# Scaling the exponentials of three attentions on GpSimd instead of on ScalarE and VectorE in turn

## The chip, the cores and the metric

The kernel runs on one core of a Trainium2 chip. The metric is the device time of one execution in microseconds (us), the median of several runs. The engines are PE (TensorE, matmuls and transposes; PEld is its weight load), DVE (VectorE), ACT (ScalarE), POOL (GpSimd) and SP (SyncE, which issues most DMAs). Each engine works through its own instructions in a fixed order and waits at semaphores for the others.

## What is computed

Two layers of a first block and one layer of a second block run over a sequence of 256 positions with 1024 features. The layers hold five kinds of softmax attention, each over 256 causal positions. What matters here is the last step of a softmax: each row of exponentials is multiplied by one factor.

```python
s = jnp.einsum('bqhd,bkhd->bhqk', qs, k).astype(jnp.float32) * scale
p = jax.nn.softmax(jnp.where(causal, s, -jnp.inf), axis=-1)
return jnp.einsum('bhqk,bkhd->bqhd', p.astype(v.dtype), v)
```

The factor is one over the sum of the row. In the second block's first attention (its branches over selected and windowed positions) it is that times a gate, `gt[:, :, 1] * o_s + gt[:, :, 2] * o_w`, which the kernel folds into the same factor.

## The kernel before

Positions lie on the 128 partitions, in two halves. The scores of one head are a tile of 128 x 384: the first 128 columns are the first 128 queries against the first 128 keys, the other 256 columns are the second 128 queries against all keys. Each half has its own row sums, so each head has two factors per partition and two multiplications, of 128 x 128 and of 128 x 256.

Heads go in pairs. For a pair, `pair_scores` (L598) makes two banks of scores on PE (L603, L612). `softmax_rows` (L314) adds the bias or mask and takes the row maximum on DVE (L315), then ACT takes the exponential and the row sums (L316). DVE makes the factors (a reciprocal at L728, L1230 or L1249, and at L1231 a product with the gates). `scaled` (L545) multiplies the exponentials with their factors in place and hands the tile to `transposed` (L578): three transposes on PE into the one bank `pt` (L271 through `tr`), and a copy to SBUF on ACT (`ptsb`, L586). `pair_values` (L555) multiplies with the values on PE (L559, L561), and `put_pair` splits the result in a high and a low part on ACT (L540) and DVE (L541).

`scaled` counts its calls in `mix`. Calls with an even count use ACT (L550), the others DVE (L552), so of each pair one head goes to DVE and the other to ACT. It is called for 48 heads: by `attend` (L716) twice in each of the first block's two layers, for three pairs each time (24 heads); in the second block's gated attention (L1218 to L1235, eight pairs, 16 heads); and in its last attention (L1240 to L1252, four pairs, 8 heads). The differential attention between (L765 to L783) does not call it.

The tile `e` of the exponentials has four buffers, `ptsb` three, `pt` one bank and the scores two banks. The scores of a pair wait until DVE has read those of the pair before (`last_read`).

Beside the attentions, the same engines prepare weights: a matmul of the projections is done in three passes with a high and a low part of each operand (`mm3`, L274 to L278), and each weight tile is split by ACT (L129) and DVE (L130). The layout library orders the instructions of each engine by priorities and its own estimates; `high_priority` blocks move scores and values ahead. The projections' and the output projection's matmuls (`acc`) fill PE between the steps of the pairs. GpSimd so far only makes reciprocal square roots (L309 to L312) and a few small clears. Its queue issues no DMA.

Of the kernel before, what the change touches and what calls it, by code (L numbers as in the profile page):

```python
# [12 lines left out]
AF = mybir.ActivationFunctionType  # L13
OP = mybir.AluOpType
# [157 lines left out]
def body(ctx: ExitStack, tc: tile.TileContext, io, out):  # L172
    nc = tc.nc
    V, A, G, T = nc.vector, nc.scalar, nc.gpsimd, nc.tensor
# [365 lines left out]
        A.activation(dst[0], src, AF.Copy)  # L540
        V.tensor_tensor(dst[1], src, dst[0].bitcast(F32), op=OP.subtract)  # L541

    mix = [0]

    def scaled(e, r, ap):  # L545

        mix[0] += 1
        for t, c in ((0, slice(0, 128)), (1, slice(128, 384))):
            if mix[0] % 2 == 0:
                A.activation(e[:, c], e[:, c], AF.Copy, scale=r[:, t:t + 1])  # L550
            else:
                V.tensor_scalar(e[:, c], e[:, c], r[:, t:t + 1], None, op0=OP.mult)  # L552
        return transposed(e, ap, False)

    def pair_values(o, pts, v, c0, first, last):  # L555
# [22 lines left out]
    def transposed(e, ap, eng):  # L578
        b = bank2()
        for i in range(3):  # L580
            tr(b[:, i * 128:(i + 1) * 128], e[:, i * 128:(i + 1) * 128])
        pt = ap.tile([128, 384], F32, tag="ptsb", name="ptsb", bufs=3)
        if eng:
            V.tensor_copy(pt, b[:, :384])
        else:
            A.activation(pt, b[:, :384], AF.Copy)  # L586
        return pt
# [27 lines left out]
    def softmax2(s, bm, ap, sm):  # L615

        e = ap.tile([128, 384], F32, tag="e", name="e", bufs=4)
        nm = small(2)
        softmax_rows(e[:, 0:128], s[:, 0:128], bm[:, 128:256], nm[:, 0:1], sm[0])
        last_read.append(softmax_rows(e[:, 128:384], s[:, 128:384], bm, nm[:, 1:2], sm[1]))  # L620
        return e
# [17 lines left out]
    def hybrid(l, xres, xT, inc, inbv, early, next_entry, hooks):  # L639
        lam0 = 0.8 - 0.6 * math.exp(-0.3 * l)  # L640
        with tc.tile_pool(name=f"at{l}", bufs=1, reuse_waits="tile") as ap:
# [74 lines left out]
            def attend(q_of, k_of, bm_of, v, k0, hook=None):  # L716

                for j in range(3):
                    if j == PUTB and hook is not None:
                        hook()  # L720
                    o = obank2()
                    hs = (2 * j, 2 * j + 1)
                    ss = pair_scores(lambda h: q_of(hs[h]), lambda h: k_of(hs[h]))
                    pts = []
                    for i, s in zip(hs, ss):
                        sm = small(4)
                        e = softmax2(s, bm_of(i), ap, (sm[:, 0:1], sm[:, 1:2]))
                        V.reciprocal(sm[:, 2:4], sm[:, 0:2])  # L728
                        pts.append(scaled(e, sm[:, 2:4], ap))
                    pair_values(o, pts, v, (64 * hs[0], 64 * hs[1]), True, True)  # L730
                    put_pair(hdT, k0 + j, o)
# [221 lines left out]
    with tc.tile_pool(name="at2", bufs=1, reuse_waits="tile") as ap:  # L953
# [264 lines left out]
        for j in range(4):  # L1218
            if j == 2:
                dq = dsa_queries()  # L1220
            o = obank2()
            T.matmul(o, vcD[:, 2 * (j % 2):2 * (j % 2) + 2, :].rearrange("p s c -> p (s c)"), cp[:, j // 2, :],
                     start=True, stop=False)
            for br in range(2):
                ss = pair_scores(lambda h: nq[64 * h:64 * h + 64, j, :], lambda h: kSW[64 * h:64 * h + 64, br, :])
                pts = []
                for h in range(2):
                    sm = small(4)
                    e = softmax2(ss[h], mask, ap, (sm[:, 0:1], sm[:, 1:2]))
                    V.reciprocal(sm[:, 2:4], sm[:, 0:2])  # L1230
                    V.tensor_tensor(sm[:, 2:4], sm[:, 2:4], gw[:, :, 8 * (1 + br) + 2 * j + h], op=OP.mult)  # L1231
                    pts.append(scaled(e, sm[:, 2:4], ap))
                    next(top, None)
                pair_values(o, pts, vSW, (128 * (1 + br), 128 * (1 + br) + 64), False, br == 1)
            put_pair(hdT, j, o)  # L1235
# [4 lines left out]
        for j in range(4):  # L1240
            o = obank2()
            ss = pair_scores(lambda h: dq[64 * h:64 * h + 64, j, :], lambda h: kD[64 * h:64 * h + 64, j, :])
            pts = []
            for sc in ss:
                sm, nm = small(4), small(2)
                e = ap.tile([128, 384], F32, tag="e", name="e", bufs=4)
                softmax_rows(e[:, 0:128], sc[:, 0:128], sel[:, 0:128], nm[:, 0:1], sm[:, 0:1])
                last_read.append(softmax_rows(e[:, 128:384], sc[:, 128:384], sel[:, 128:384], nm[:, 1:2], sm[:, 1:2]))
                V.reciprocal(sm[:, 2:4], sm[:, 0:2])  # L1249
                pts.append(scaled(e, sm[:, 2:4], ap))  # L1250
            pair_values(o, pts, vD, (128 * j, 128 * j + 64), True, True)
            put_pair(hdT, 4 + j, o)  # L1252
# [117 lines left out]
```

## Time and profile before

| | |
|---|---|
| median of three runs | 978.37 us (977.81 to 980.41) |
| the profiled execution | 977.63 us |
| its span, first to last instruction | 975.8 us |
| PE busy | 944.4 us (97%) |
| DVE busy | 650.5 us (67%) |
| ACT busy | 533.2 us (55%) |
| POOL busy | 29.2 us (3%), 54 instructions |
| mean granted TensorE clock | 0.993 |

The profiled execution took 0.74 us less than the median, and 1.83 us lie outside its span. A busy share is an average over stages with different limits. Matmuls are pipelined, so a busy PE is not a PE at its peak: a matmul's record lasts longer than the distance to the next one's start. A row of the view by stretches gives, for each engine, the busy time and the number of its instructions (x) within that stretch; a row of the timeline gives start, duration, engine, line, operation, tiles, shape and, in brackets, the idle time before it and what ended that.

### The profile page before, as it was taken

How to read it: one execution, taken by the hardware profiler on the slowest of the kernel's cores; microseconds unless marked ns; L12 is line 12 of the kernel's file. 1: busy time of each engine (PE TensorE's matmuls, PEld its weight loads, DVE VectorE, ACT ScalarE, POOL GpSimd, SP SyncE). 2: the span in 40 equal slices, each digit the busy share in tenths (PEclk: the TensorE clock that was granted, in tenths of full speed). 3: DMA queues.
4: the chain of work that ended last, by engine and by line, in shares of the span. 5: the costliest groups of instructions: out<-in, count | busy, mean ns of one | idle time of the engine just before them, and what ended most of it. 6: DMA issues, size and time to landing. Idle time of an engine off the chain costs nothing. (4 is left out here: it accounts for less than half of the span.)

```text
span 975.8 us, 16344 instructions
## 1 busy us (share of the span) xinstructions
PE 944.4 (97%) x6378; PEld 834.9 (86%) x6378; DVE 650.5 (67%) x1367; ACT 533.2 (55%) x1023; POOL 29.2 (3%) x54
## 2 busy tenths in 40 slices
PE   8999999999999999999999999889999899999997
PEld 6888689999998888878999999788666699999996
DVE  4648687767678757767767464787688665454543
ACT  4658665444444677655444444555599744344542
POOL 0000000000000100000000000101000100000000
PEclk9999999999999999999999999999999999999999
DMA  8745548877875533447875565365312156555441
GB/s 313 288 100 215 196 176 301 300 278 270 300 254 175 192 131 127 149 179 278 308 277 211 177 242 190 109 242 206 130 45 87 65 173 215 175 181 205 153 153 44
DMA packets 33456, 190.55 MB, mean 195 GB/s; under 512 B 3696, under 2 KB 5346, under 8 KB 15842
## 3 DMA queue, kind: packets, MB, share of 16 engines
q1 hardware_dynamic: 31224, 183.75, 52.9%
q10 hardware_dynamic: 2154, 5.75, 2.0%
q8 instruction: 50, 0.82, 0.3%
q14 instruction: 28, 0.23, 0.1%
HBM read 188.17 MB, written 1.32 MB: 194 GB/s over the span
## 5 line engine op out<-in xcount | busy, mean ns | idle before, releaser
L130 DVE TENSOR_TENSOR lo<-raw,hi 128x1024 fp32r<-128x1024 f32 (+3 forms) x284 | 339.1, 1202 | 99.7 <-ACT hi L129 95.6
L129 ACT ACTIVATE hi<-raw 128x1024 fp32r<-128x1024 f32 (+3 forms) x284 | 293.7, 1041 | 103.1 <-PE acc L278 52.3
L278 PE MATMUL sc<-xh,lo 128*128 128x256 f32 x960 | 271.8, 283 | 0.0
L276 PE MATMUL sc<-xh,hi 128*128 128x256 f32 x960 | 271.7, 283 | 0.0
L277 PE MATMUL sc<-xl,hi 128*128 128x256 f32 x960 | 271.7, 283 | 0.0
L276 PEld LDWEIGHTS sc<-xh,hi 128*128 128x128 f32 x960 | 184.2, 192 | 1.1
L277 PEld LDWEIGHTS sc<-xl,hi 128*128 128x128 f32 x960 | 184.2, 192 | 1.0
L278 PEld LDWEIGHTS sc<-xh,lo 128*128 128x128 f32 x960 | 184.2, 192 | 0.0
L276 PE MATMUL acc<-hi,xh 128*128 128x512 f32 (+4 forms) x384 | 135.2, 354 | 0.4 <-ACT hi L129 0.3
L277 PE MATMUL acc<-lo,xh 128*128 128x512 f32 (+4 forms) x384 | 134.0, 349 | 0.7 <-DVE lo L130 0.6
L278 PE MATMUL acc<-hi,xl 128*128 128x512 f32 (+4 forms) x384 | 133.6, 349 | 0.7 <-DVE xl L298 0.7
L276 PE MATMUL acc<-hi,hh 128*128 128x512 f32 x264 | 103.2, 391 | 0.0
L277 PE MATMUL acc<-lo,hh 128*128 128x512 f32 x264 | 103.2, 391 | 0.0
L278 PE MATMUL acc<-hi,hl 128*128 128x512 f32 x264 | 102.8, 389 | 0.0
L453 ACT ACTIVATE sg<-sc 128x256 f32<-128x256 f32 x60 | 22.6, 376 | 137.9 <-PE sc L278 137.9
L455 DVE TENSOR_TENSOR hm<-sc,sg 128x256 f32<-128x256 f32 x60 | 25.3, 421 | 88.0 <-ACT sg L453 88.0
L276 PEld LDWEIGHTS acc<-hi,xh 128*128 128x128 f32 x384 | 74.4, 194 | 8.5 <-issue 1.5
L277 PEld LDWEIGHTS acc<-lo,xh 128*128 128x128 f32 x384 | 74.4, 194 | 6.7 <-DVE lo L130 1.6
L278 PEld LDWEIGHTS acc<-hi,xl 128*128 128x128 f32 x384 | 74.2, 194 | 6.9 <-DVE xl L298 2.0
L316 ACT ACTIVATE e<-e,sm 128x128 f32<-128x128 f32 (+1 forms) x128 | 56.8, 446 | 12.0 <-DVE sm L315 7.7
L278 PEld LDWEIGHTS acc<-hi,hl 128*128 128x128 f32 x264 | 49.6, 188 | 10.8 <-DVE hl L457 0.2
L276 PEld LDWEIGHTS acc<-hi,hh 128*128 128x128 f32 x264 | 49.7, 188 | 9.8 <-ACT hh L456 0.3
(277 smaller groups left out, 1155.7 us busy)
## 6 DMA issues: line engine op xcount, KB each, us to landing
raw<-in_w_gate SPq DMA_DIRECT2D x33, 1024.0 KB, 4.9
raw<-in_w_up SPq DMA_DIRECT2D x33, 1024.0 KB, 4.9
raw<-in_w_down SPq DMA_DIRECT2D x33, 1024.0 KB, 5.0
ada<-in_w_ada SPq DMA_DIRECT2D x48, 512.0 KB, 5.2
raw<-in_w_o SPq DMA_DIRECT2D x8, 1024.0 KB, 5.2
raw<-in_w_inaqk SPq DMA_DIRECT2D x6, 1024.0 KB, 5.1
raw<-in_w_inbqk SPq DMA_DIRECT2D x4, 1024.0 KB, 6.2
gb<-in_lnrows ACTq DMA_DIRECT2D x4, 1024.0 KB, 6.2
```

Of the source, the lines that this page charges most:

```text
L129: self.nc.scalar.activation(hi[:, :n], t[:, c], AF.Copy)
L130: self.nc.vector.tensor_tensor(lo[:, :n], t[:, c], hi[:, :n].bitcast(F32), op=OP.subtract)
L276: T.matmul(dst, lh, rh, start=start, stop=False)
L277: T.matmul(dst, lh, rl, start=False, stop=False)
L278: T.matmul(dst, ll, rh, start=False, stop=stop)
L316: A.activation(e, e, AF.Exp, bias=nm, scale=-1.0, accum_out=sm)
L453: A.activation(sg, pg[:, 0, :], AF.Silu)
L455: V.tensor_tensor(hm, pg[:, 1, :], sg, op=OP.mult)
```

## The change

The alternation goes. All 96 multiplications are done by GpSimd, with the same tiles, in place, in the same two pieces.

```diff
-    mix = [0]
-
     def scaled(e, r, ap):
 
-        mix[0] += 1
         for t, c in ((0, slice(0, 128)), (1, slice(128, 384))):
-            if mix[0] % 2 == 0:
-                A.activation(e[:, c], e[:, c], AF.Copy, scale=r[:, t:t + 1])
-            else:
-                V.tensor_scalar(e[:, c], e[:, c], r[:, t:t + 1], None, op0=OP.mult)
+            G.tensor_scalar(e[:, c], e[:, c], r[:, t:t + 1], None, op0=OP.mult)
         return transposed(e, ap, False)
```

The instructions of the attentions are ordered anew; in the feed-forward parts the order stays. Three places show it. Line numbers of the changed kernel are six lower behind `scaled`, so L586 is L580, L603 is L597, L612 is L606, L559 is L553 and L561 is L555 there; its multiplication is L546.

ACT in the gated attention, from the exponentials of the second head on. Before:

```order
L550 ACTIVATE e<-e,sm 128x128
L550 ACTIVATE e<-e,sm 128x256
L316 ACTIVATE e,sm<-e,sm 128x128
L586 ACTIVATE ptsb<-pt 128x384
L316 ACTIVATE e,sm<-e,sm 128x256
L316 ACTIVATE e,sm<-e,sm 128x128
L586 ACTIVATE ptsb<-pt 128x384
L316 ACTIVATE e,sm<-e,sm 128x256
L129 ACTIVATE hi<-raw 128x1024
L550 ACTIVATE e<-e,sm 128x128
L550 ACTIVATE e<-e,sm 128x256
L586 ACTIVATE ptsb<-pt 128x384
```

The same place in the changed kernel:

```order
L316 ACTIVATE e,sm<-e,sm 128x128
L316 ACTIVATE e,sm<-e,sm 128x256
L580 ACTIVATE ptsb<-pt 128x384
L316 ACTIVATE e,sm<-e,sm 128x128
L316 ACTIVATE e,sm<-e,sm 128x256
L129 ACTIVATE hi<-raw 128x1024
L316 ACTIVATE e,sm<-e,sm 128x128
L580 ACTIVATE ptsb<-pt 128x384
L316 ACTIVATE e,sm<-e,sm 128x256
L316 ACTIVATE e,sm<-e,sm 128x128
L316 ACTIVATE e,sm<-e,sm 128x256
L580 ACTIVATE ptsb<-pt 128x384
```

The multiplications are gone from ACT, and the copy of a transposed head stands behind the exponentials of one or two later heads.

PE in the first layer's first attention, from a pair's scores on. Before:

```order
L603 MATMUL sc<-kT,qT 128x128 x2
L612 MATMUL sc<-kT,qT 128x256 x2
L271 MATMUL pt<-cst,e 128x128 x3
L603 MATMUL sc<-kT,qT 128x128 x2
L612 MATMUL sc<-kT,qT 128x256 x2
L271 MATMUL pt<-cst,e 128x128 x3
L276 MATMUL acc<-xh,hi 128x256
```

The same place in the changed kernel:

```order
L597 MATMUL sc<-kT,qT 128x128 x2
L606 MATMUL sc<-kT,qT 128x256 x2
L271 MATMUL pt<-cst,e 128x128 x3
L276 MATMUL acc<-xh,hi 128x256
L277 MATMUL acc<-xl,hi 128x256
L276 MATMUL acc<-xh,hi 128x256
L277 MATMUL acc<-xl,hi 128x256
L278 MATMUL acc<-xh,lo 128x256
L271 MATMUL pt<-cst,e 128x128 x3
```

Between the transposes of a pair's two heads, five matmuls of a projection now stand where the next pair's scores stood; those scores have moved behind the second transposes.

POOL in the gated attention, where before it had no instruction:

```order
L546 TENSOR_SCALAR e<-e,sm 128x128
L546 TENSOR_SCALAR e<-e,sm 128x256
L546 TENSOR_SCALAR e<-e,sm 128x128
L546 TENSOR_SCALAR e<-e,sm 128x256
L546 TENSOR_SCALAR e<-e,sm 128x128
```

All heads stand one behind the other on one engine, 96 such rows in the whole program, with nothing else between them inside an attention.

## Rows read from the trace of the kernel before

**Rows 1.** By stretches, three stretches in attentions; all engines' busy time.

```profile
98.00:118.00 20.00, 18.45 (x110) 12.70 (x109) 13.67 (x45) 14.31 (x41) 0.00 (x0) 1.00 0.48 161
360.00:377.00 17.00, 16.80 (x125) 13.20 (x124) 13.13 (x54) 16.18 (x51) 0.00 (x0) 1.00 0.18 63
712.00:758.00 46.00, 44.66 (x291) 28.79 (x290) 39.09 (x197) 42.65 (x138) 0.00 (x0) 1.00 0.24 79
```

**Rows 2.** The multiplications, by line, whole run: ns shortest/median/longest.

```profile
L550 ACT ACTIVATE e<-e,sm x48: 384/448/512, 61.8 to 761.2; 128x128 f32<-128x128 f32 x24, 128x256 f32<-128x256 f32 x24
...
L552 DVE TENSOR_SCALAR e<-e,sm x48: 268/316/352, 60.9 to 758.9; 128x128 f32<-128x128 f32 x24, 128x256 f32<-128x256 f32 x24
```

**Rows 3.** Stretch 712 to 758, multiplications alone: L550 on ACT, L552 on DVE.

```profile
712.00:758.00 46.00, 8.31 (x21) 1.00 0.24 79
...
712.00:758.00 46.00, 5.42 (x20) 1.00 0.24 79
```

**Rows 4.** Stretch 712 to 758, PE by line: L276, L271, L603, L559, L1222.

```profile
712.00:758.00 46.00, 9.46 (x22) 4.17 (x22) 1.00 0.24 79
...
712.00:758.00 46.00, 11.93 (x66) 6.95 (x65) 1.00 0.24 79
...
712.00:758.00 46.00, 5.40 (x40) 3.30 (x40) 1.00 0.24 79
...
712.00:758.00 46.00, 5.87 (x36) 1.78 (x36) 1.00 0.24 79
...
712.00:758.00 46.00, 1.89 (x6) 0.90 (x6) 1.00 0.24 79
```

**Rows 5.** Timeline of PE, one pair of the last attention, 751.36 to 754.67.

```profile
751.36 0.49 PE L603 MATMUL sc<-kD,dq 64*128 64x128 f32 x4
...
752.22 0.55 PE L271 MATMUL pt<-cst,e 128*128 128x128 f32 x3
752.52 0.48 PE L277 MATMUL acc<-lo,xh 128*128 128x512 f32 x1
752.84 0.40 PE L278 MATMUL acc<-hi,xl 128*128 128x512 f32 x1
753.07 0.39 PE L276 MATMUL acc<-hi,xh 128*128 128x512 f32 x1
...
753.87 0.65 PE L559 MATMUL ob<-ptsb,vD 128*64 128x256 f32 x4 [0.18 <-ACT ptsb L586]
...
754.67 0.38 PE L603 MATMUL sc<-kD,dq 64*128 64x128 f32 x2
```

**Rows 6.** Groups of POOL by shape: xcount | busy us, mean ns | idle before.

```profile
L309 POOL TENSOR_SCALAR sm<-sm 128x8 f32<-128x8 f32 x2 | 0.5, 246 | 118.2 <-DVE sm L791 118.2
L1026 POOL MEMSET y<- 128x32 f32 x2 | 0.3, 128 | 22.8 <-PE pt L271 22.8
...
L1359 POOL MEMSET const-float32-1.0<- 128x1 f32 x1 | 0.1, 98 | 0.0
```

**Rows 7.** Timeline of POOL, four multiply-or-add instructions of one column.

```profile
121.59 0.31 POOL L311 TENSOR_SCALAR sm<-sm 128x1 f32<-128x1 f32 x1 [24.23 <-ACT acc L523]
...
130.47 1.00 POOL L311 TENSOR_SCALAR sm<-sm 128x1 f32<-128x1 f32 x1 [7.92 <-ACT acc L523]
...
673.29 0.22 POOL L309 TENSOR_SCALAR sm<-sm 128x1 f32<-128x1 f32 x1 [12.43 <-ACT y L958]
...
774.78 0.30 POOL L311 TENSOR_SCALAR sm<-sm 128x1 f32<-128x1 f32 x1 [2.87 <-ACT acc L897]
```

**Rows 8.** Timeline of DVE beside two of those.

```profile
129.98 1.41 DVE L529 SCALAR_TENSOR_TENSOR y<-y,sm,gb 128x512 f32<-128x512 f32 x2
...
774.49 0.69 DVE L920 TENSOR_TENSOR y<-acc,gm 128x512 f32<-128x512 f32 x1
```

**Rows 9.** Stretch 712 to 758, DVE by line: L130, L1231.

```profile
712.00:758.00 46.00, 7.31 (x6) 1.00 0.24 79
...
712.00:758.00 46.00, 2.15 (x14) 1.00 0.24 79
```

## The prediction

> **What bounds the kernel now.** I read the table of engines first: PE is busy for 97% of the span, so the question is where PE only looks busy. The view by stretches answers that. Rows 1 hold three attention stretches; the one from 712 to 758 us, in the second block's gated attention and the first pairs of its last one, stands out [rows 1]: of its 46.0 us ACT is busy for 42.65 and DVE for 39.09, and POOL does nothing. PE shows 44.66, but a record of PE is longer than the distance to the next start, so I price PE by starts. In one pair [rows 5] the scores take 0.86 us (751.36 to 752.22), a head's three transposes 0.30 (752.22 to 752.52), a projection's matmul 0.23 (752.84 to 753.07), and the values 0.80 (753.87 to 754.67). The stretch has 22 matmuls of L276 and as many of each of its two sisters, 66 transposes, 40 records of L603 (four to a pair, ten pairs), 36 of L559 (four to a pair, nine pairs) and 6 of L1222 [rows 4]. That is 66 x 0.23 = 15.2, 66 x 0.10 = 6.6, 10 x 0.86 = 8.6, 9 x 0.80 = 7.2, and 6 x 0.23 = 1.4 with the last taken like a projection's matmul: 39.0 us. So PE could leave this stretch 7 us earlier, and ACT, with 3.35 us idle in 46, is the engine that holds it. In the first block's stretches PE is the fuller engine or close to it, and ACT has either much room (14.31 of 20.0) or little (16.18 of 17.0) [rows 1].
>
> **The change part by part.**
>
> *Removed from ACT and DVE.* Over the run ACT loses 48 instructions of 448 ns in the median and DVE 48 of 316 ns [rows 2]: 21.5 and 15.2 us of records. In the stretch they occupy 8.31 us of ACT and 5.42 us of DVE [rows 3]. ACT falls from 42.65 to 34.3 us and DVE from 39.09 to 33.7. Neither has anything else to take over from POOL.
>
> *Added to POOL.* 96 multiplications, of 128 and of 256 columns. No row of the trace shows one so wide. From below: a one-column instruction of this operation takes 0.22 us [rows 7], and a clear of 32 columns takes 128 ns against 98 for one [rows 6], so 0.97 ns a column, without a read; a head then costs 0.34 + 0.47 = 0.81 us. From above: the same operation with 8 columns takes 246 ns [rows 6] against 0.22 us, 3.6 ns a column, over seven columns only; that makes 0.68 + 1.14 = 1.82 us. I take 1.1 us a head, nearer the lower end, because the row of the clear reaches over 31 columns and that of the operation over so few that its slope may be fixed cost. The Trainium skill, GPSIMD Engine Reference, section Performance versus the Vector engine, gives 1.8 cycles an element at 1.2 GHz as the best case of such a loop; by that, an estimate, a head costs 1.0 us and the sum below stays as it is. In the stretch there are 41 halves of heads [rows 3], 20.5 heads, so 22.6 us of POOL's idle 46: it is not the fullest engine.
>
> *The new longest in the stretch.* PE's 39.0 us. If it keeps beside it the 3.35 us that ACT left idle, the stretch takes 42.35 instead of 46.0: 3.65 us less. The bounds are 0 (the steps of a pair wait for each other as before) and 7.0 (PE alone). I take 3.6.
>
> *The wait within a pair.* The two heads of a pair were multiplied on two engines; now they stand in one queue, and what is queued behind the first is the second, then the next pair. PE's transposes wait for it, behind them the projection's matmuls, and ACT's copy with the exponentials that stand behind that. The exponentials of the two heads are themselves one behind the other on ACT, so a second head that comes later than the first by as much as POOL needs for one head waits for nothing. At 1.1 us that is nearly so, and the order puts five matmuls between the two transposes in the first layer. Outside the stretch there are about 27 heads, 24 of them in the four attentions of the first block. There I cost the step at nothing, the cover being those matmuls. Without cover each of those 12 pairs pays about 0.6 us, 7 in all; from below, the stretch from 360 to 377, where ACT fills 16.18 of 17.0 us, and its like in the other three could give back 1 us each, 4 in all.
>
> *The moved scores.* In the first layer's first attention the next scores stand behind the second transposes instead of ahead of them. That delays them by about five matmuls and one set of transposes and is hidden by the same projection; bounds 0 and 1 us for that attention. No DMA is issued by the moved step, and POOL's own work in an attention (the reciprocal roots) lies outside the pairs.
>
> *The port between DVE and POOL.* A one-column instruction of L311 takes 0.31 us at 121.59 and 1.00 us at 130.47 [rows 7]; at 130.47 DVE was in two instructions of L529, whose two tensors lie in SBUF, until 131.39 [rows 8], and POOL ended 0.08 us later. Beside L920, which reads one operand from PSUM, the same instruction takes 0.30 [rows 7, 8]. So POOL waits for DVE's instructions with two SBUF tensors. In the stretch these are 6 splits of L130 with 7.31 us together and 14 small products of L1231 [rows 9]. POOL has 23 us to spare for the splits. Whether DVE waits in turn for POOL no row shows; the bounds are 0 and the length of one instruction, some 0.6 us, for each of the 20. I take 0 for the sum.
>
> *Sum.* -3.6 us. The profiled execution took 977.63 us with a span of 975.8; it would take 974.0. It stood 0.74 us below the median of the runs shown, 978.37, so the median becomes **974.8 us**.
>
> **The rivals.** A measurement of this kernel can tell about 0.3% from no change, 2.9 us: faster means below 975.4, slower above 981.3.
>
> *The port gives the gain back: 978.4.* If DVE also waits for POOL, a product of L1231 that should take 0.15 us stands behind a multiplication, and with it the factors of the next head. POOL would be busy for half the stretch, so half of the 20 instructions would meet it and wait 0.3 us on the mean: 3 us on DVE, which lies in the chain of each pair, plus up to 0.7 us (1.00 less 0.31) for a POOL that waits for a split. That cancels 3.6. For it: the row at 130.47. Against it: the row at 121.59 and its like, and that DVE keeps room. The Trainium skill, SBUF — State Buffer, section Who interferes with whom, states it as a rule: an instruction of VectorE with two SBUF inputs and one of GpSimd that reads SBUF exclude each other, and the later one blocks for the whole of the earlier. By that rule this rival holds; the trace agrees for one direction, with 1.00 us against 0.31.
>
> *GpSimd is too slow for a pair: 988.* At the upper price of 1.82 us a head, a pair needs 3.64 us in one queue, where two engines side by side needed no more than 0.9 us (two instructions of 448 ns). The stretch then holds 20.5 x 1.82 = 37.3 us of POOL plus its waits for the splits, up to 7.3: 44.6, and with the 3.35 idle 48.0, so 2 us more than now. In the 12 pairs of the first block the second head comes about 1.8 - 1.1 = 0.7 us later than in my sum, and with the cover already spent each pays that once: 8 us. Together 10 more than now, 988. It decides from about 1.4 us a head on. For it: the slope between one and eight columns. Against it: the clear's.
>
> *More than the stretch gains: 970.* If the PE floor is nearly reached (7 us instead of 3.6) and the stretches of the first block give 1 us or so, the sum is -8. For it: 16.18 of 17.0 us on ACT. Against it: PE's waits are fixed hops between engines, of which the change removes none.
>
> That the change doesn't do what it says I exclude: the order of the built program has the 96 multiplications on POOL and none on ACT or DVE, and the tiles lie in SBUF.
>
> **How the numbers follow.** Forecast 0.40, more gain 0.10, the port 0.27, the slow GpSimd 0.23. Part of the forecast's own spread reaches into "no change" and part of the port's case into a gain; they about balance. Chances: faster 0.48, within 0.3% 0.28, slower 0.24. The range goes from 968.5, a little beyond the largest gain, to 987, near the slow case: outside lie the wider half of the slow case and a few hundredths of the large gain, under 0.2 in all. The likeliest case by itself has 971 to 977.
>
> **What the changed profile would show.** Right: POOL busy for about 29 + 53 = 82 us; its 128 x 256 instruction near 0.65 us and its 128 x 128 near 0.45; the stretch from the compressed branch's end to the output projection some 3 to 4 us shorter; ACT near 80% in it; the first block's attentions as long as before. Wrong: waits of PE's transposes for POOL in the list of waits, over 3 us in all; DVE's small products lasting half a microsecond; or POOL above 100 us. If the second block's attentions keep their length although POOL is cheap, the bound was not ACT but the chain from a pair's scores to its values, and the step that fails is that the idle 3.35 us stays the same.

## The result and the profile after

The changed kernel takes **992.17 us** (median of four runs, 991.19 to 993.24) against 978.39 us for the kernel before beside it: a ratio of **1.0129** (95% interval 1.0114 to 1.0144). It is 13.8 us slower. The forecast was 974.8 us with a range from 968.5 to 987, so sign and range both missed. The profiled execution took 992.88 us, 991.1 of them in its span.

The table of engines of the changed kernel, and GpSimd's multiplications by shape: over the whole run, then in a stretch in which DVE did not hold it up, 66.5 to 73.6 us (count | busy us, mean ns of one | idle before).

```profile
PE 952.2 (96%) x6378; PEld 838.1 (85%) x6378; DVE 640.9 (65%) x1319; ACT 518.4 (52%) x975; POOL 111.6 (11%) x150
...
L546 POOL TENSOR_SCALAR e<-e,sm 128x256 f32<-128x256 f32 x48 | 51.4, 1071 | 0.0
L546 POOL TENSOR_SCALAR e<-e,sm 128x128 f32<-128x128 f32 x48 | 32.7, 681 | 122.8 <-DVE sm L722 60.2 <-DVE sm L1225 38.5 <-PE sc L606 18.4
...
L546 POOL TENSOR_SCALAR e<-e,sm 128x256 f32<-128x256 f32 x3 | 2.8, 924 | 0.0
L546 POOL TENSOR_SCALAR e<-e,sm 128x128 f32<-128x128 f32 x3 | 1.8, 604 | 4.1 <-DVE sm L722 3.0 <-PE ob L555 1.1
```

A head costs 0.60 + 0.92 = 1.53 us when nothing disturbs GpSimd (a pair of records started together reads 1.50), and (51.4 + 32.7) / 48 = 1.75 us in the mean. That is not the 1.1 us of the forecast; it lies near the upper bound that [rows 6] and [rows 7] gave, 1.82.

Next, where the time went. The timeline of PE gives marks that both kernels pass: the first scores of layer 0 (`kT,qT`), of layer 1, and of the second block (`kSW,nq`), the last values of the gated attention (`vSW`) and of the last one (`vD`). Before:

```profile
42.83 0.49 PE L603 MATMUL sc<-kT,qT 96*128 96x128 f32 x2
...
352.10 0.42 PE L603 MATMUL sc<-kT,qT 96*128 96x128 f32 x2
...
702.54 0.48 PE L603 MATMUL sc<-kSW,nq 64*128 64x128 f32 x2
...
749.01 0.39 PE L561 MATMUL ob<-ptsb,vSW 128*64 128x128 f32 x4
...
767.17 0.39 PE L561 MATMUL ob<-ptsb,vD 128*64 128x128 f32 x4
```

And the same marks in the changed kernel:

```profile
43.90 0.49 PE L597 MATMUL sc<-kT,qT 96*128 96x128 f32 x2
...
364.92 0.43 PE L597 MATMUL sc<-kT,qT 96*128 96x128 f32 x2
...
719.64 0.48 PE L597 MATMUL sc<-kSW,nq 64*128 64x128 f32 x2
...
766.82 0.39 PE L555 MATMUL ob<-ptsb,vSW 128*64 128x128 f32 x4
...
782.09 0.39 PE L555 MATMUL ob<-ptsb,vD 128*64 128x128 f32 x4
```

| from ... to | before | after | change |
|---|---|---|---|
| start to layer 0's first scores (no multiplication yet) | 42.8 | 43.9 | +1.1 |
| to layer 1's first scores | 309.3 | 321.0 | **+11.7** |
| to the second block's first scores | 350.4 | 354.7 | +4.3 |
| gated attention | 46.5 | 47.2 | +0.7 |
| last attention | 18.2 | 15.3 | **-2.9** |
| to the end of the span | 208.6 | 209.0 | +0.4 |

The sum is +15.3, which is the difference of the spans. The first line is the scatter of the start (it lies between -0.3 and +1.1 in the runs below). Most of the loss is in layer 0. The second block gains 2.2 us, but not in the gated attention, on which the forecast's gain rested. That stretch, which stands here from 729 to 775, has lost its multiplications on ACT and DVE, and its length has not followed:

```profile
729.00:775.00 46.00, 44.87 (x298) 28.37 (x298) 37.53 (x181) 37.66 (x122) 34.61 (x43) 1.00 0.24 80
```

The columns are those of [rows 1]. ACT is down from 42.65 to 37.66 us and DVE from 39.09 to 37.53, less than to the 34.3 and 33.7 of the forecast, in part because one more weight is split within the stretch; PE's work is the same.

In layer 0 the three attentions follow each other: the first (`kT`, `vC`), the differential one (`kB`, `vB`), which `scaled` does not touch, and the dilated one (`qkA`, `vA`). The view by stretches from 101 us on shows the dilated one; PEclk is the third number from the end. Before:

```profile
101.00:108.00 7.00, 6.62 (x43) 4.33 (x43) 5.61 (x22) 5.85 (x19) 0.00 (x0) 1.00 0.75 261
108.00:115.00 7.00, 6.63 (x41) 4.48 (x40) 4.31 (x14) 6.08 (x17) 0.00 (x0) 1.00 0.33 113
115.00:122.00 7.00, 7.00 (x33) 5.79 (x32) 3.52 (x10) 2.03 (x5) 0.33 (x2) 1.00 0.82 302
```

After:

```profile
101.00:108.00 7.00, 3.74 (x16) 2.60 (x15) 4.39 (x11) 3.09 (x7) 3.96 (x3) 0.86 0.24 101
108.00:115.00 7.00, 4.68 (x19) 2.50 (x20) 2.47 (x11) 3.60 (x14) 3.78 (x4) 0.50 0.42 149
115.00:122.00 7.00, 6.82 (x36) 4.04 (x32) 2.88 (x14) 3.90 (x16) 2.62 (x4) 0.67 0.00 1
```

From 101 to 115 us PE does 35 matmuls where it did 84, and no engine is full: the engines wait for each other in turn. In the middle of that the granted clock falls to 0.50, its level of 1.2 GHz, where it was 1.00 before. The list of waits of the changed kernel from 84 to 126 us names the step (us in total, times, longest):

```profile
ACT ptsb L580 <- PE pt L271: 10.1, 7, 3.4
PEld pt L271 <- POOL e L546: 7.2, 7, 2.5
PE pt L271 <- POOL e L546: 5.0, 5, 2.0
```

PE's transposes wait for the multiplications, ACT's copy for the transposes. PEld's row is largely the same time as PE's, so PE itself stands for 5.0 us. What stands behind the waiting instruction is the rest of the answer. PE of the changed kernel, with GpSimd and DVE beside it:

```profile
103.69 0.39 PE L278 MATMUL acc<-hi,xl 128*128 128x512 f32 x1
106.12 0.47 PE L271 MATMUL pt<-cst,e 128*128 128x128 f32 x1 [2.05 <-POOL e L546]
107.80 0.69 PE L271 MATMUL pt<-cst,e 128*128 128x128 f32 x2 [1.21 <-POOL e L546]
108.42 0.80 PE L597 MATMUL sc<-qkA 64*128 64x128 f32 x4
...
105.45 2.29 POOL L546 TENSOR_SCALAR e<-e,sm 128x128 f32<-128x128 f32 x2 [2.71 <-DVE sm L722]
...
105.12 0.16 DVE L722 RECIPROCAL sm<-sm 128x2 f32<-128x2 f32 x1
...
105.74 1.22 DVE L130 TENSOR_TENSOR lo<-raw,hi 128x1024 fp32r<-128x1024 f32 x1
```

The same place before:

```profile
99.36 0.49 PE L603 MATMUL sc<-qkA 64*128 64x128 f32 x4 [0.81 <-DVE sm L315]
...
100.22 0.55 PE L271 MATMUL pt<-cst,e 128*128 128x128 f32 x3
```

In the changed kernel there is nothing for PE between the projection's matmul at 103.69 and the first head's transposes, and the scores of the *next* pair (108.42) stand behind those transposes. Before, they stood ahead of them. So the second pair's softmax cannot start while GpSimd works on the first head. GpSimd's two instructions at 105.45 took 2.29 us instead of 1.50, because DVE's split of a weight, two tensors in SBUF, ran from 105.74 to 106.96. Of PE's first wait, 2.05 us up to 106.12, GpSimd's work fills only the last 0.67: it began at 105.45, when DVE had made the head's factor (105.12), 1.8 us after ACT had the row sums, with a weight's split and another product ahead of it in DVE's queue. Before, that factor came 2.2 us after its sums, but PE had projections to do meanwhile.

### The profile page after: what moved, and what is told of

It reads as the page before. It is cut to its first block, busy times and chain, and to the rows that moved or that the text cites. A ratio compares the mean times of both kernels' runs of the same rounds, so it can differ in the third digit from the quotient of the medians.

```text
span 991.1 us, 16462 instructions
## 1 busy us (share of the span) xinstructions
PE 952.2 (96%) x6378; PEld 838.1 (85%) x6378; DVE 640.9 (65%) x1319; ACT 518.4 (52%) x975; POOL 111.6 (11%) x150
## 5 line engine op out<-in xcount | busy, mean ns | idle before, releaser
L130 DVE TENSOR_TENSOR lo<-raw,hi 128x1024 fp32r<-128x1024 f32 (+3 forms) x284 | 339.4, 1203 | 106.2 <-ACT hi L129 101.1
L276 PE MATMUL sc<-xh,hi 128*128 128x256 f32 x960 | 271.7, 283 | 0.0
L276 PEld LDWEIGHTS sc<-xh,hi 128*128 128x128 f32 x960 | 184.2, 192 | 1.1
L276 PE MATMUL acc<-hi,xh 128*128 128x512 f32 (+4 forms) x384 | 135.8, 356 | 0.4 <-ACT hi L129 0.4
L276 PE MATMUL acc<-hi,hh 128*128 128x512 f32 x264 | 103.2, 391 | 0.0
L546 POOL TENSOR_SCALAR e<-e,sm 128x128 f32<-128x128 f32 x96 | 82.5, 876 | 122.8 <-DVE sm L722 60.2
L276 PEld LDWEIGHTS acc<-hi,xh 128*128 128x128 f32 x384 | 74.9, 196 | 8.4 <-ACT hi L129 1.4
L311 POOL TENSOR_SCALAR sm<-sm 128x1 f32<-128x1 f32 x16 | 8.9, 554 | 626.2 <-ACT acc L523 420.0
```

What stands on the lines that cost most here:

```text
L130: self.nc.vector.tensor_tensor(lo[:, :n], t[:, c], hi[:, :n].bitcast(F32), op=OP.subtract)
L276: T.matmul(dst, lh, rh, start=start, stop=False)
L546: G.tensor_scalar(e[:, c], e[:, c], r[:, t:t + 1], None, op0=OP.mult)
```

## The experiments

The heads are counted in the order of the program: 1 to 6 are layer 0's first attention, 7 to 12 its dilated one, 13 to 24 those of layer 1, 25 to 40 the gated attention, 41 to 48 the last one. The first runs change only where GpSimd multiplies. They start from the kernel before, and HERE is the condition that each of them names; elsewhere the heads take turns at ACT and DVE:

```diff
         for t, c in ((0, slice(0, 128)), (1, slice(128, 384))):
-            if mix[0] % 2 == 0:
+            if mix[0] % 2 == 0 and not (HERE):
                 A.activation(e[:, c], e[:, c], AF.Copy, scale=r[:, t:t + 1])
             else:
-                V.tensor_scalar(e[:, c], e[:, c], r[:, t:t + 1], None, op0=OP.mult)
+                (G if HERE else V).tensor_scalar(e[:, c], e[:, c], r[:, t:t + 1], None, op0=OP.mult)
```

Ratios are to runs of the kernel before on the same chip, whose medians lay between 978.6 and 980.0 us. "Layer 0 loses" is the second line of the table above: first scores to first scores, less 309.3 us.

**Which block.** HERE is `mix[0] <= 24`, then `mix[0] > 24`.

> GpSimd multiplies in the first block's four attentions alone (24 heads); the second block takes turns at ACT and DVE as before. Theory (price in series): a head costs GpSimd 1.5 us alone and 1.75 in the mean, the two heads of a pair stand in one queue, and TensorE stands at the transposes, worst in layer 0's dilated attention, where its clock then falls. The trace of the change has lost 15.2 us when layer 1's attentions are over, and nothing of it lies in the second block: about 993.5 us (991 to 996), with a stretch at the 1.2 GHz level near 106 us. Rival (port): DVE and POOL block each other wherever both work, so the 13.8 us divide as the heads do, 0.29 us a head: 24 heads give about 985.

> GpSimd multiplies in the second block's two attentions alone (24 heads). Theory (price in series): ACT and DVE are the fuller engines there, and the second block's attentions take about 2 us less, as they did in the change (65.1 to 62.9 us): 976.5 us (975 to 978.5). Rival (port): 0.29 us lost a head, 985. My prediction's own figure for this part was -3.6 us: 974.8.

The first gave 992.57 us, 1.0138 (1.0123 to 1.0154); layer 0 loses 11.7, as in the change. The second gave 977.69 us, 0.9989 (0.9978 to 1.0001). So all of the loss comes from the first block, and the second gains about a microsecond by the ratio, whose interval reaches 1, and 2.4 in the trace. A loss spread over all heads is excluded.

**Which attention of layer 0.** HERE is `not 7 <= mix[0] <= 12` (all but the dilated one), then `7 <= mix[0] <= 12` (it alone).

> GpSimd multiplies everywhere but in the six heads of layer 0's dilated attention, which take turns at ACT and DVE as before. Theory (price in series, and the clock with it): the 9.5 us that the change lost between 94.5 and 117 us go away, TensorE's clock stays up there, the rest stays: about 982.5 us (980 to 985). Rival (port): 42 of 48 heads keep their 0.29 us: 990.5. Rival (the scheduler's new order, not the duration): the order changes most in layer 0's first attention, which stays on GpSimd here: 990 or more.

> The counterpart: GpSimd multiplies only the six heads of layer 0's dilated attention. Theory (price in series, and the clock with it): these three pairs alone cost 8 to 10 us, far more than the 3 x 3 us by which their multiplications are longer could cost at an unchanged clock, and the clock's records fall to the 1.2 GHz level near 105 us: 987 us (985 to 989). If the clock does not fall, 3 pairs x 1.5 us = 4.5 us: 983. Rival (port): 6 x 0.29 = 1.7 us, 980.

986.58 us, 1.0077 (1.0062 to 1.0092), and 982.14 us, 1.0036 (1.0022 to 1.0050). Both expectations missed by 4 to 5 us, in a telling way: without GpSimd in the dilated attention layer 0 still loses 6.0 us, and with GpSimd there alone it loses 3.9. So about half of layer 0's loss is caused by the six heads of its first attention, and the two halves do not quite add up to 11.7. The later runs follow that up.

**The price.** HERE is `mix[0] % 2 == 0` (the second head of each pair; DVE keeps the first), then `t == 1` (the 256 columns of every head).

> GpSimd multiplies the second head of every pair, VectorE the first, as before; ScalarE none. The price of a head on GpSimd stays 1.5 us, but no head stands behind another there. Theory (two heads in series): what remains is a second head about 0.6 us later than by ScalarE (1.5 less 0.9) in the first block's 12 pairs, of which layer 0's six pay, and the second block gains 2 us: 980 us (976 to 983), and the clock falls near 106 us for no more than 3.4 us. Rival (the price of a head alone counts, not the series): half of what the change lost in the first block stays, 985 or more.

> GpSimd multiplies the 256 columns of a head's second half, the 128 of its first half stay with ScalarE and VectorE by turns: 0.9 us a head on GpSimd alone, less than the 1.1 us that my prediction assumed, so this shows whether the prediction's claim for a cheap GpSimd was right. Theory (price): at this price the first block loses little, and the second gains: 979 us (975 to 982). Rival (a third engine in each head's chain costs, whatever its price): the first block keeps over half of its loss, 985 or more.

The second head alone gave 985.68 us, 1.0057 (1.0037 to 1.0076): over the range of my theory, and what the rival gave. Layer 0 loses 5.1 us. Two heads in one queue are not needed for a loss. The wide piece alone gave 978.51 us, 0.9995 (0.9979 to 1.0010), layer 0 loses -0.1, and GpSimd's row reads:

```profile
L552 POOL TENSOR_SCALAR e<-e,sm 128x256 f32<-128x256 f32 x48 | 45.8, 958 | 147.1 <-DVE sm L728 63.3 <-DVE sm L1231 46.2 <-PE sc L612 18.3
```

All 48 heads pass through GpSimd here, in pairs, at 0.96 us each, and the first layer pays nothing (layer 1, up to the second block, still 3.2 us, and the second block gives 1.6 back). So the loss goes with GpSimd's time for a head: layer 0 loses nothing at 0.96 us, 5.1 us where every second head costs (27.2 + 17.8) / 24 = 1.88 in the mean, and 11.7 where every head costs 1.75. (The library orders each of these kernels anew, so the time acts through its order as well as through the waits.) The run with the second heads had these rows:

```profile
L552 POOL TENSOR_SCALAR e<-e,sm 128x256 f32<-128x256 f32 x24 | 27.2, 1135 | 0.0
L552 POOL TENSOR_SCALAR e<-e,sm 128x128 f32<-128x128 f32 x24 | 17.8, 741 | 154.8 <-DVE sm L728 83.1 <-DVE sm L1231 49.6 <-PE ob L561 5.7
```

**The clock.** The changed kernel, with eight transposes of a constant (`mask`) ahead of each head's own in layer 0's dilated attention, which write over them.

```diff
-        return transposed(e, ap, False)
+        mix[0] += 1
+        return transposed(e, ap, False, 8 * (7 <= mix[0] <= 12))
...
-    def transposed(e, ap, eng):
+    def transposed(e, ap, eng, fill=0):
         b = bank2()
+        for _ in range(fill):
+            tr(b[:, 0:128], mask[:, 0:128])
```

> The changed kernel, and in layer 0's dilated attention eight transposes of a constant ahead of each head's own, written over by it: 48 x 0.1 us of TensorE work that waits for nothing, in its idle time. Theory (the clock doubles the cost): TensorE is less idle, its granted clock stays up near 106 us or comes back sooner, and up to half of the 13.7 us at the 1.2 GHz level, some 5 us, come back: 988 us (985 to 991). Rival (only the wait for GpSimd counts, the clock fell beside it): 992 to 997, the transposes' own time on top where TensorE was not idle.

990.90 us, 1.0110 (1.0091 to 1.0129), at the edge of the expected range. The view by stretches:

```profile
101.00:108.00 7.00, 4.26 (x22) 2.83 (x21) 4.17 (x16) 3.84 (x13) 4.30 (x5) 0.92 0.15 63
108.00:115.00 7.00, 7.00 (x49) 5.81 (x48) 4.15 (x17) 4.34 (x18) 5.01 (x7) 0.83 0.45 151
115.00:122.00 7.00, 6.73 (x51) 5.21 (x50) 1.73 (x3) 3.13 (x7) 2.91 (x4) 1.00 0.01 2
```

The clock lacks 0.08 + 0.17 of 7 us here, where it lacked 0.14 + 0.50 + 0.33 in the change: a quarter. Layer 0 loses 10.1 instead of 11.7 us, although PE makes 48 transposes more. But the order changed with the edit: the next pair's scores, which stand behind all three transposes of the first head in the change, stand here behind one of them.

```profile
105.66 0.33 PE L271 MATMUL pt<-cst,e 128*128 128x128 f32 x1 [2.74 <-POOL e L548]
105.92 0.49 PE L606 MATMUL sc<-qkA 64*128 64x128 f32 x4
...
106.78 0.59 PE L271 MATMUL pt<-cst,e 128*128 128x128 f32 x2
```

So the run does not separate the clock from the order, and how much of the 1.6 us is the clock's is not shown.

**Held-back matmuls.** In the order of the change, 73 projection matmuls stand between the differential attention's first and last scores (34 before) and 41 between the dilated attention's first scores and its last values (85 before). The next run keeps more for the dilated one: its third query and key projection is made to wait for the first pair's scores.

```diff
+                        if k == 0 and behind is not None:
+                            tc.add_manual_dep(m.ins, behind.ins.name,
+                                              mybir.DependencyInfo(mybir.DependencyClass.Sync, mybir.DependencyReason.DATA),
+                                              reason="late")
...
+            project(0)
+            project(1)
+            if not late:
+                project(2)
...
-            attend(lambda i: half(qA, i), lambda i: half(kA, i), lambda i: bias[:, i, :], vA, 0, putB)
+            attend(lambda i: half(qA, i), lambda i: half(kA, i), lambda i: bias[:, i, :], vA, 0, putB, (lambda m: project(2, (0, 1), m)) if late else None)
```

The second run has the same hold without GpSimd in the dilated attention, the third is the kernel before with the hold.

> The changed kernel, with the last of the three query and key projections of layer 0's dilated attention held behind the scores of that attention's first pair: 81 projection matmuls stand between its first scores and its last values, as against 41 in the change and 85 before. Theory (the work that hides the wait was spent too early): in the change the slow first attention pulled 40 projection matmuls, 9 us of TensorE, ahead into itself and the differential attention; kept for the dilated one, they cover part of GpSimd's time there, and layer 0 loses about 6.5 us instead of 11.8, with a clock that falls for 3.4 us at most: 987 us (984.5 to 989.5). Rival (only the sum of the projection work counts; what is kept here is missing in the differential attention): 991 to 993.

> The same hold, with layer 0's dilated attention on ACT and DVE by turns (the earlier run without GpSimd there, plus the hold): 89 projection matmuls in that attention instead of 43. No multiplication of GpSimd lies in it, so what layer 0 lost there, 3.8 us of 6.0, can only come from the moved projections. Theory (spent too early): these 3.8 us come back, the clock does not fall near 106 us: 983 us (981 to 984.5). Rival (sum of the projection work): 986 to 987.5, as without the hold.

> Control: the kernel before with the same hold, no work on GpSimd: 96 projection matmuls instead of 85 in the dilated attention. Both theories: the hold by itself costs nothing, 978.5 us (977 to 980). If it costs or gains more than 1.5 us, the two runs with the hold have to be read against this one.

997.96 us, 1.0197 (1.0181 to 1.0212); 992.47 us, 1.0140 (1.0123 to 1.0157); control 979.87 us, 1.0017 (1.0006 to 1.0029). **Both theories fell**, and both rivals with them: the kernels with the hold take about 6 us more than the same kernels without it, of which the control explains 1.3. The first run's stretches show why:

```profile
80.00:87.00 7.00, 2.52 (x16) 1.39 (x14) 6.81 (x28) 3.98 (x13) 0.00 (x0) 0.82 0.63 197
87.00:94.00 7.00, 7.00 (x31) 5.03 (x31) 3.97 (x20) 3.39 (x16) 0.00 (x0) 0.50 0.25 104
94.00:101.00 7.00, 7.00 (x32) 6.35 (x31) 0.92 (x2) 0.49 (x1) 0.00 (x0) 0.50 0.00 0
```

The hole moves into the differential attention (PE busy for 2.52 of 7 us), the clock falls there, and the matmuls that were held back are then done at half of it. The differential attention itself, which GpSimd never touches, takes 18.2 us from its first to its last scores with the hold, 16.5 in the change and 12.4 before. With fewer projection matmuls between them its pairs are no earlier, so these matmuls filled a gap and did not make it. What makes the pairs late?

**The buffers of the exponentials.** The tile `e` has four buffers, two pairs. The next run gives the first block a fifth (`held_e[0]` is 5 there and 4 in the second block), with room from two small tiles; the other is the kernel before with the same edit.

```diff
-        e = ap.tile([128, 384], F32, tag="e", name="e", bufs=4)
+        e = ap.tile([128, 384], F32, tag="e", name="e", bufs=held_e[0])
...
-                    r = ap.tile([128, 3, 32], F32, tag="rt", name="rt", bufs=2)
+                    r = ap.tile([128, 3, 32], F32, tag="rt", name="rt", bufs=1)
...
-            lp = ap.tile([128, 64], F32, name="lp")
+            lp = ap.tile([128, 2, 32], F32, tag="kr", name="lp", bufs=2).rearrange("p a b -> p (a b)")
```

> The changed kernel with five buffers for the exponentials in the first block instead of four (room from one rotation buffer and a shared one). Theory (buffers): an exponential is held from ScalarE's write to its transposes, longer by GpSimd's 1.5 us a head, and the next pair's softmax waits for it; with one more buffer the differential attention comes back towards 12.4 us from 16.5, and about 4 of the 11.8 us that layer 0 lost come back: 988 us (985.5 to 990). Rival (the order on TensorE): the differential attention stays above 15 us, 991 to 993.

> Control: the kernel before with five buffers for the exponentials. Both theories: its pairs are not held up by buffers much, 978 us (976 to 979.5).

986.34 us, 1.0069 (1.0054 to 1.0084), and for the control 979.06 us, 0.9997 (0.9987 to 1.0008). One buffer takes half of the loss away, and it is worth nothing where GpSimd does not multiply. Layer 0 loses 5.3 instead of 11.7. My theory named the wrong place, though: the differential attention still takes 15.7 us; the dilated one, first scores to last values, falls from 32.2 to 26.9 (27.9 before). Its timeline of PE with five buffers:

```profile
103.59 0.49 PE L603 MATMUL sc<-qkA 64*128 64x128 f32 x4 [0.92 <-DVE sm L315]
...
105.27 0.33 PE L271 MATMUL pt<-cst,e 128*128 128x128 f32 x1 [0.75 <-POOL e L548]
```

And its view by stretches:

```profile
101.00:108.00 7.00, 4.61 (x26) 2.82 (x24) 5.43 (x19) 4.43 (x16) 4.87 (x5) 1.00 0.07 28
108.00:115.00 7.00, 5.89 (x40) 3.65 (x40) 3.75 (x14) 4.94 (x17) 3.83 (x6) 1.00 0.42 151
```

The next pair's scores (103.59) stand ahead of the first head's transposes (105.27) again, the two pairs overlap, and the clock stays at 1.00. That a buffer more brings this order back is shown. Why the layout library puts the scores behind with four is inferred: by its own estimates the tiles stay taken for as long as GpSimd needs. A DVE that stood still for a buffer at that moment is not among the waits.

The order alone is not what costs. In the run without GpSimd in the dilated attention the scores stand behind the first head's transposes as well:

```profile
105.20 0.61 PE L271 MATMUL pt<-cst,e 128*128 128x128 f32 x3 [1.75 <-DVE e L552]
105.75 0.59 PE L603 MATMUL sc<-qkA 64*128 64x128 f32 x4
```

Its clock falls there too (0.65 from 108 to 115 us), and yet that attention takes 26.9 us against 32.2, with 43 projection matmuls in it against 41. With five buffers it takes 26.9 with 47. So, as far as these two runs go, taking away either the moved scores or GpSimd's time there gives about 5 us back. Nor does a loss need the moved scores: with the second heads alone on GpSimd the scores stand ahead (102.24, the transposes from 103.10), and layer 0 loses 5.1 us.

**The pair before the differential attention.** HERE is `not 5 <= mix[0] <= 6`, then `not 5 <= mix[0] <= 12`.

> GpSimd multiplies everywhere but in the last pair of layer 0's first attention (2 heads of 48, by ACT and DVE in turn). Theory (order on TensorE, or the buffers that this pair holds): the differential attention's second scores come early again, it takes about 13 us instead of 16.5, and layer 0 loses some 7 instead of 11.8 us: 987.5 us (985.5 to 989.5). Rival (every pair adds its own delay alike): a twelfth of the first block's loss comes back, 991.

> GpSimd multiplies neither in that last pair nor in layer 0's dilated attention. Compared with the run without GpSimd in the dilated attention alone (986.6 us, 6.0 us lost in layer 0), two more heads go back to ACT and DVE. Theory (that pair sets the differential attention back): layer 0 loses 2 us, and the clock does not fall near 106 us: 982 us (980 to 984). Rival (every pair alike): 4 us, 985.

987.89 us, 1.0087 (1.0071 to 1.0104): as the theory had it, with a differential attention of 13.3 us and 6.8 us lost in layer 0. One pair of 24 makes a third of the loss, so pairs do not count alike. The second gave 984.66 us, 1.0048 (1.0033 to 1.0063), the rival's 985 and not the theory's 982: layer 0 still loses 5.3 us with GpSimd in only four of its heads, and the dilated attention, without GpSimd, takes 30.5 us. From 90.2 to 121 us:

```profile
90.20:121.00 30.80, 28.13 (x147) 19.85 (x146) 19.46 (x61) 17.96 (x48) 1.91 (x2) 0.89 0.29 101
```

The clock lacks 0.11 of that stretch. The order that the library makes from there on differs in every one of these kernels, and how much of the 5.3 us is that order and how much the clock stays open.

**The second block.** HERE is `mix[0] > 24 and mix[0] % 2 == 0` (the second heads; ACT has none left), then `mix[0] > 40` (the last attention).

> As the run before, but in the second block alone; the first block is that of the kernel before. Theory (two heads in series): ScalarE, the fullest engine there, is relieved of all its multiplications without a second head that waits: 2.5 us off or a little more, 976 us (974 to 977.3). Rival (the relief does not count, the hops between engines do): 978 to 979, as before.

> GpSimd multiplies only in the second block's last attention (8 heads); the gated one, the stretch on which my forecast of a gain rested, and the first block are those of the kernel before. With GpSimd in the whole second block the trace gained 0.5 us up to the start of the last attention's second half and 1.5 behind it. Theory (the gain sits at the end, where the chain of a pair stands without other work, and the fullness of ScalarE in the gated attention does not set its length): 977 us (975.8 to 978.2). Rival (ScalarE and VectorE bound the gated attention, and the gain is made there): 978.4, as before.

978.67 us, 0.9989 (0.9978 to 1.0000), and 978.52 us, 0.9999 (0.9988 to 1.0010): both theories missed, and both rivals' figures came. From the block's first scores to its last values the traces show 63.5 and 63.3 us, against 64.7 before and 62.4 with GpSimd for all 24 heads. The medians cannot tell these differences from nothing; the marks within the traces can. In the five kernels whose second block multiplies as before, the gated attention takes 46.4 to 46.5 us and the last one 18.2. With GpSimd in the last one alone these are 46.4 and 16.7; with GpSimd in both they are 46.9 to 48.3 and 15.2 to 15.3, in every run. So the small gain sits in the last attention, as the second run's theory had it, though its 1.5 us did not come in the median; the gated one only loses.

**Two versions without the loss.** GpSimd in the second block and five buffers in the first; then the wide piece everywhere and five buffers.

> GpSimd multiplies in the second block alone, and the first block has five buffers for the exponentials. Theory: the second block gives back its 2 us, the fifth buffer, which changed nothing in the control (0.9997), adds at most half a us: ratio 0.998, about 977 us against 979 (the ratio between 0.9965 and 0.9992). Rival (both effects lie within the scatter): ratio 1.000.

> The 256 columns of each head on GpSimd, the 128 by turns on ACT and DVE, and five buffers for the exponentials in the first block. Without the fifth buffer this was 0.9995, with 1.7 us lost in layer 1's attentions and 1.4 gained in the second block. Theory (price and buffers): the fifth buffer takes the loss in layer 1 away, ratio 0.998 (0.9965 to 0.9995). Rival (the loss in layer 1 is the order's or the clock's, not the buffers'): 0.9995 or above.

977.63 us, **0.9985** (0.9974 to 0.9996): about 1.5 us faster than before, the only run whose interval lies below 1, and 14 us faster than the change. The gain is below the 0.3% that I counted as a difference. The wide piece gave 978.58 us, 0.9996 (0.9986 to 1.0005), the rival's value: the fifth buffer does not free a gain there.

## Why the prediction was wrong

*The price of a head.* "I take 1.1 us a head, nearer the lower end, because the row of the clear reaches over 31 columns and that of the operation over so few that its slope may be fixed cost." This is the step that failed first. The slope is (924 - 604) / 128 = 2.5 ns a column, between the clear's 0.97 and the operation's 3.6, and nearer the operation: its row was the same operation, the clear reads nothing. The Trainium skill, GPSIMD Engine Reference, section Performance versus the Vector engine, gives 1.8 cycles an element at 1.2 GHz as the best case; the rows show 3.0, and the estimate of 1.0 us a head that I drew from it agreed with my choice and was wrong with it.

*The wait within a pair.* "There I cost the step at nothing, the cover being those matmuls", with bounds from -4 to +7. At 0.96 us a head that is what layer 0 showed. At 1.5 to 1.75 PE's transposes wait for GpSimd 5.0 us from 84 to 126 us alone, and layer 0 loses 11.7 us. The upper bound was too low, because each pair was priced by itself. A late pair makes the next one late: one pair taken back gave about 4 us and a shorter differential attention. That this adds up over all pairs until the cover ends is how I read the traces; no run tests it.

*The moved scores.* "That delays them by about five matmuls and one set of transposes and is hidden by the same projection; bounds 0 and 1 us for that attention." I had looked at one attention. The same move in the dilated one, with GpSimd's time in front of the scores, takes away the overlap of two pairs, and a fifth buffer, with which the scores come first again, gave 6.4 of layer 0's 11.7 us back. The sign of the danger stood in the order of the program; I read it as a detail.

*A term that was missing.* The granted clock did not occur in the sum. From 101 to 122 us it lacks 0.97 of a stretch of 7 us (what that cost is not shown, see above), and near 655 us the clock falls for a moment more often than before:

```profile
651.00:658.00 7.00, 3.79 (x17) 3.15 (x16) 6.16 (x10) 2.44 (x6) 1.02 (x2) 0.83 0.56 185
658.00:665.00 7.00, 7.00 (x40) 6.88 (x40) 5.21 (x13) 4.73 (x8) 0.00 (x0) 0.93 0.89 320
```

That is about (0.17 + 0.07) x 7 = 1.7 of the 4.3 us up to the second block, in a stretch that holds no multiplication and reads 1.00 before. Eight of the eighteen runs show such a fall there, none of them with the first block of the kernel before. One of them has GpSimd in layer 0's dilated attention alone and still loses 1.9 us from layer 1's first scores on, where it multiplies nothing. What decides whether the clock falls there was not tested.

*The gain.* "PE's 39.0 us. If it keeps beside it the 3.35 us that ACT left idle, the stretch takes 42.35 instead of 46.0: 3.65 us less." It did not shrink: the gated attention takes 47.2 us instead of 46.5 with ACT 5 us emptier. ACT was not the bound, and PE's 39.0 us were too few. I took 0.23 us for each of the 66 projection matmuls; [rows 5] has 0.32 for the one behind the transposes (752.52 to 752.84), and from each start to PE's next the 66 take 20.5 us in the stretch, not 15.2. The ten pairs' scores take 10.2 and not 8.6. PE's records leave 1.3 us of the stretch free before (44.66 of 46.0) and 1.1 after (44.87). That points to PE itself as the bound, and not to the chain from a pair's scores to its values, which the text had named for this case; no run decides between the two. The last attention gave 2.9 us, of which I had counted only the first pairs.

*The rivals.* "GpSimd is too slow for a pair" was the right one, at 988. Its threshold of 1.4 us a head fits the runs (nothing in layer 0 at 0.96, a loss at 1.75), its place, the first block's pairs, too; its 8 us were too few for the reasons above, and its +2 us in the second block had the wrong sign. The port was half right. GpSimd waits for DVE: 1.75 instead of 1.50 us a head. DVE hardly waits for GpSimd, as its splits show (last section) and its small products (count of 16 | busy, mean ns, in the second block's attentions):

```profile
L1225 DVE TENSOR_TENSOR sm<-sm,gw 128x2 f32<-128x2 f32 x16 | 3.0, 190 | 0.1
```

That is 0.6 us more in all than the 2.4 us of the same 16 before, not the 3 us that the rival needed.

*The signs.* POOL at 111.6 us lies above the 100 that I named as a sign of being wrong, and PE's waits for POOL, 6.7 us over the run, above 3. Both were in the list, and both came.

## What to carry to other kernels

Where a slower engine takes over a step between two rotating buffers, price it over the chain of pairs and not pair by pair, and look in the new order for the next pair's first step behind the slow one: that is where an overlap is lost, and one more buffer may bring it back. For an operation that the trace shows only in a small shape, take the slope from the same operation, not from a cheaper one, and let the forecast hang on a threshold that can be run by itself (half the width on the slow engine would have told it). In a stretch in which PE's cover ends, a wait is followed by work at the lower clock (four scores took 0.80 us there, 0.49 before); how much of the loss that makes stays open here. An edit that is meant to test one cause can move the order too: compare the order of every test kernel before reading its time.

## What the runs showed of the hardware

GpSimd's multiplication by a factor per partition takes 0.60 us for 128 and 0.92 us for 256 float32 columns, and a head 2.29 or 2.46 us instead of 1.50 beside a DVE instruction with two SBUF tensors. At 75.05 DVE's split of a weight began 0.45 us later:

```profile
72.06 1.50 POOL L546 TENSOR_SCALAR e<-e,sm 128x128 f32<-128x128 f32 x2 [1.27 <-DVE sm L722]
75.05 2.46 POOL L546 TENSOR_SCALAR e<-e,sm 128x128 f32<-128x128 f32 x2 [1.49 <-DVE sm L750]
...
75.50 1.22 DVE L130 TENSOR_TENSOR lo<-raw,hi 128x1024 fp32r<-128x1024 f32 x1
```

Over the whole run 12 of the 96 multiplications take 1.1 to 2.0 us. Beside each of them a split was running that had begun before it or in its first 0.04 us; none of the other 84 had one. In the other direction, 14 splits began inside a multiplication that had 0.16 to 0.85 us to go; 13 of them took 1.20 to 1.29 us and one 1.47, where the median of all is about 1.22.

The Trainium skill, SBUF — State Buffer, section Who interferes with whom, has the later one of such a pair wait for the whole of the earlier; the row at 105.45 agrees for GpSimd, whose second piece ends 0.8 us after DVE's split. For DVE it does not: the same split began 0.29 us into GpSimd's first piece of 0.6 us and took its usual 1.22.

A matmul that waits for nothing is not free of risk when it is moved. Held back by a few microseconds, it left a hole in which PE was busy for 2.52 of 7 us, the clock fell to its 1.2 GHz level, and layer 0 lost 19.1 us instead of 11.7.
